# Splitting the tokens for the expert gather inside the routing stage, on ScalarE and VectorE

## The chip, the cores and the metric

The kernel runs on one core of one Trainium2 chip. The metric is the device time of one execution in microseconds (us); three runs of the kernel before took 749.75, 750.12 and 750.17, median 750.12. Beside them stands one execution taken with the hardware profiler, from which all durations below are read. Times in rows count from the start of its span.

The engines are named TensorE (PE in the rows; PEld is its weight load), VectorE (DVE), ScalarE (ACT), GpSimd (POOL) and SyncE (SP). SyncE issues nearly all transfers; they run on 16 DMA engines.

## The reference

One decoder layer on 256 tokens of width 1024, in float32. First a mixer (two attention branches of 8 heads, gates, an output projection), then the part that the change is in, a mixture of 64 experts with hidden width 256, of which each token takes 8:

```python
h2 = modulate(rms_norm(x, norm2_g), shift2, scale2)      # 256 x 1024 tokens
scores = sigmoid(h2 @ w_router)                          # 256 x 64
choice = scores + router_bias
# 4 of 8 groups by the sum of their two best, then the 8 best experts in them
wts = scores at the chosen experts, normalised, times 2.5
y[token] = sum over its 8 experts of
           wts * (silu(h2 @ w_gate_e) * (h2 @ w_up_e)) @ w_down_e
y += swiglu of the shared expert, on all tokens
x = x + gate2 * y
out = rms_norm(x, final_g)
```

Each expert has three matrices of 1 MB, 64 x 3 MB in all, and each must be read once.

## The kernel before, in words

The kernel has three stretches. The mixer runs to about 240 us. The routing stage follows, in which the tokens are normalised, scored and assigned, and the shared expert's first product is formed. Then comes the expert stage, 26 tiles of 128 slots each.

A tile holds the slots of two experts (64 + 64, or 96 + 32) or of four (32 each). The first three tiles take experts 0 to 5, whose weights can be loaded before the routing is known; the later tiles take experts in the order of their counts, and their loads read the expert's number from the tensor `order`, which SyncE loads into registers (line 1093). For each tile there are a matrix `S` of ones and zeros, token by slot (`slots`, line 1039, made on VectorE by comparing places), a gather of the tokens (`gather`, line 1058), the gate and up product (`tile_up`, line 1122, into the one PSUM buffer `gu`), a turn of the hidden values (`hidden_T`), the down product (`down`, line 1169) and the scatter into the four accumulators (line 1185). The scatter and the next gather stand between a tile's gate and up product and its down product; in tile 0 the next gather stands behind the down product.

The gather is a matrix product of tokens with `S`. From tile 1 on it runs in bfloat16, on three parts of each token that add up to it: `hp3[t][0]`, `[1]` and `[2]` for the two halves t of the 256 tokens. Part 0 is h2 rounded, part 1 the rounded rest, part 2 the rest of the rest. `part` (line 1031) makes them, a copy on ScalarE and a subtraction on GpSimd in each of four calls; the rest lies in the buffer `sr` (`r1`). h2 itself lies in the buffer `gr0` and is read there in steps of eight elements. Tile 0's gather takes h2 in float32 instead, with `S` in float32, so that it needs no parts: 32 products instead of 48.

The weights go into a ring of 1 MB buffers, `ring` (line 121 and 798). `w8()` takes the next name in it; each expert takes three: half of gate and up, the other half, and down. The ring begins with vv and the nine w8 buffers; then come whi, whi, wlo, wlo, hh, g2r, xs and gr1, buffers of the mixer and the routing that come free one after the other, and before tile 3 gr0 and sr are put in front (line 1272). In the rows gr0 and gr1 both read `gr`. The shared expert takes the first two, tiles 0, 1 and 2 the next 18.

The order of work on TensorE, VectorE, ScalarE and SyncE is the order of the program text (`manual_schedule`, line 194): an engine executes its instructions in that order, and waits at the first one whose inputs or whose buffer are not ready. In the mixer a list of steps, `plan`, gives that order. SyncE's queue holds the loads in the order of the tiles, and a load whose buffer is in use holds all that are behind it. Beside that each load waits until an earlier one has landed.

In the routing stage, from line 1205, the shared expert's products (`shared_up`) are cut into pieces between the steps of the routing: `choose` picks the experts of one half of the tokens (VectorE), `places` counts the slots (TensorE, then VectorE), `rank` and `expert_order` make `order`, `choice_weights` the weights. `residual` copies x into the accumulators on ScalarE, after which xs is free.

Of the kernel before, what the change touches and what calls it, by code (L numbers as in the profile page):

```python
# [21 lines left out]
NT = 2  # L22
# [86 lines left out]
def block_kernel(ctx: ExitStack, tc: tile.TileContext, x, c, norm1_g, norm2_g, w_ada, b_ada, w_in,  # L109
# [63 lines left out]
    def tokens_T(t, place):  # L173

        for half in range(2):
            p = place()
            for b in range(4):
                nc.tensor.transpose(p[:, b * 128:(b + 1) * 128], h2v[t][:, 4 * half + b, :], ident)
            nc.scalar.activation(h2T[0][:, half * 4:half * 4 + 4, t * 128:(t + 1) * 128],
                                 p.rearrange("p (b q) -> p b q", b=4), AF.Copy)  # L180

    lgs = {}
# [12 lines left out]
    with ExitStack() as pa:  # L195
# [473 lines left out]
        def channel_tiles():  # L669
            h = k8("gr0", [P, NT, D])  # L670
            h2.extend(h[:, t] for t in range(NT))
            h2v.extend(h[:, t].rearrange("q (p j) -> q j p", j=8) for t in range(NT))
            r1.extend(a.rearrange("p (j q) -> p j q", j=8) for a in (sr[:, 0], sr[:, 1]))
            h2T.append(k8("gr1", [P, 8, 256]))
            pack = k8("qksb3", [P, 4, NT, NE])
            scores_.extend(pack[:, i] for i in range(4))
# [4 lines left out]
        def do(f, *args, keys=()):  # L681
            plan.append((keys, lambda: f(*args)))
# [95 lines left out]
        do(outp, 1, 0, 1)  # L778
        do(tokens_T, 0, att)
        do(outp, 1, 4, 1)  # L780
        do(router, 0, att)
# [16 lines left out]
    ring.insert(0, "vv")  # L798
    ring.extend(["whi", "whi", "wlo", "wlo", "hh", "g2r", "xs", "gr1"])
    hp3.extend([k8(f"qk{n}{k}", [P, 8, P], BF) for k in range(3)] for n in ("sb", "mb"))  # L800
    ps = ctx.enter_context(tc.tile_pool(name="ps2", bufs=1, reuse_waits="tile", space=PSUM))
# [228 lines left out]

    def part(t, k):

        src = h2v[t] if k == 0 else r1[t]
        nc.scalar.activation(hp3[t][k], src, AF.Copy)
        nc.gpsimd.tensor_tensor(hp3[t][2] if k else r1[t], src, hp3[t][k], op=OP.subtract)

    xgb = []

    def slots(i, dtype=BF):

        entries = TILES[i]
        S = wk.tile([P, NT, 128], dtype, name="S", tag="zs", bufs=4)
        for t in range(NT):
# [14 lines left out]
    def gather(i, S):  # L1058
        if not xgb:
            xgb.append(k8("hl", [P, 2, 8, 128]))  # L1060
        xg = xgb[0][:, i % 2]

        parts = h2v if i == 0 else [hp3[t][k] for t in range(NT) for k in range(3)]
        n = len(parts)
        for half in range(2):
            p = rot()
            for b in range(4):
                for k in range(n):
                    mm(p[:, b * 128:(b + 1) * 128], parts[k][:, half * 4 + b, :], S[:, k * NT // n], start=k == 0,  # L1069
                       stop=k == n - 1)  # L1070
            dst = xg[:, half * 4:half * 4 + 4].rearrange("p b s -> p (b s)")
# [132 lines left out]

    load_shared()
    shared_up(0, 0, 5)
    tokens_T(1, rot)
# [3 lines left out]
    scores(1)  # L1211
    choose(0)
    choose(1)
    nc.scalar.preload_act_table_set("silu_and_others")
    for t in range(NT):
        for half in range(2):
            residual(t, half)
    shared_up(1, 0, 2)
    places()
    S = slots(0, F32)  # L1220
    shp[0] = swiglu(shp[0])
    shared_up(1, 2, 8)
    shp[1] = swiglu(shp[1])
    xg = gather(0, S)
    part(0, 0)
    part(1, 0)
    rank()
    expert_order()
    choice_weights()
    part(0, 1)  # L1230
    part(1, 1)

# [37 lines left out]
    for i in range(len(TILES)):  # L1270
        if i == 3:
            ring[:0] = ["gr0", "sr"]
        if i == SH_AT:
# [58 lines left out]
```

## Time and profile before

| | |
|---|---|
| median of three runs | 750.12 us (749.75 to 750.17) |
| the profiled execution, its own time | 748.62 us |
| its span, first to last instruction | 746.5 us |
| mean granted clock of TensorE | 0.987 of full |
| TensorE busy | 696.3 us, 93% of the span |
| VectorE busy | 312.3 us, 42% |
| ScalarE busy | 202.3 us, 27% |
| GpSimd busy | 25.1 us, 3% |
| DMA | 266.73 MB, mean 357 GB/s |
| chain that ended last | TensorE 53%, DMA 41%, VectorE 2%, ScalarE 1% |

A row of the timeline gives a start, a busy time, the engine, the line of the kernel, and what is written from what; the brackets at its end tell how long the engine sat idle before, and whom it waited for. TensorE's busy time is no measure of how near it is to its peak, since matmuls are pipelined. The engine with the most busy time doesn't bound every stage: in the routing stage one reads which wait ends last. SPq is SyncE's queue; a row there is the issue of a transfer, not the transfer.

### The profile page before, as it was taken

To read this page: it belongs to the slowest core of one execution; us is meant where nothing else is said; L and a number is where in the kernel's file an instruction comes from. 1 tells how busy PE (TensorE), PEld (TensorE's weight loads), DVE (VectorE), ACT (ScalarE), POOL (GpSimd) and SP (SyncE) were. 2 spreads that over 40 slices of the span, in tenths; PEclk is the share of its full clock that TensorE was granted. 3 is DMA by queue.
4 is the path that set the end of the run, shared out by engine and by line. 5 is a ranking of instruction groups with operands and counts; after the bars stand their busy time and mean duration, and the time that the engine had idled before them with its cause. 6 is when DMAs were issued, how large, how long until landed. Compare 5 with 4: busy or idle time off the path is not lost.

```text
span 746.5 us, 12489 instructions
## 1 busy us (share of the span) xinstructions
PE 696.3 (93%) x4727; PEld 389.5 (52%) x4727; DVE 312.3 (42%) x663; ACT 202.3 (27%) x332; POOL 25.1 (3%) x37
## 2 busy tenths in 40 slices
PE   3799999999999979999999999999999998899994
PEld 0486677667787645544444444444444453445532
DVE  1365766766667342333333233332242332223323
ACT  2354665465743231111111111011111110111122
POOL 1010001000001050000000000000000000000000
PEclk9999999999999998999999999999999999999998
DMA  9999988776658659999999999999999999999994
GB/s 352 412 380 389 375 285 301 253 270 217 240 210 297 250 216 383 375 382 413 409 414 413 413 410 396 411 411 412 415 412 412 413 412 414 406 410 412 406 333 157
DMA packets 76862, 266.73 MB, mean 357 GB/s; under 512 B 7013, under 2 KB 9221, under 8 KB 67968
## 3 DMA queue, kind: packets, MB, share of 16 engines
q1 hardware_dynamic: 75344, 262.24, 90.9%
q0 software_dynamic: 1312, 3.65, 1.5%
q8 instruction: 39, 0.64, 0.3%
q14 instruction: 23, 0.19, 0.1%
q10 hardware_dynamic: 144, 0.00, 0.0%
HBM read 264.68 MB, written 1.19 MB: 356 GB/s over the span
## 4 chain that ended last, share of the span: by engine, by line
PE 53%; DMA 41%; DVE 2%; ACT 1%; SPq 1%; issue 1%; POOL 1%; DVEq 0%; ACTq 0%
PE gu L1129 9%; PE big L264 7%; PE big L267 7%; PE big L265 7%; DMA w<-in_w_up_e_dram 6%; DMA w<-in_w_gate_e_dram 5%; DMA whi<-in_w_gate_e_dram 5%; PE rot L1069 5%; PE rot L1153 4%; DMA w<-in_w_ada_dram 3%; DMA whi<-in_w_down_e_dram 3%; PE acc L1185 3%; DMA g2r<-in_w_gate_e_dram 3%; DMA vv<-in_w_down_e_dram 2%; PE att L412 2%; DMA g2r<-in_w_up_e_dram 2%
## 5 line engine op out<-in xcount | busy, mean ns | idle before, releaser
L1129 PE MATMUL gu<-w,hl 128*32 128x512 f32 (+1 forms) x552 | 108.1, 594 | 1.5 <-DMA w<-in_w_up_e_dram 1.4
L264 PE MATMUL big<-whi,hh 128*128 128x512 f32 x184 | 75.0, 408 | 1.7 <-ACT whi L384 1.7
L1153 PE MATMUL rot<-w,at 128*32 128x512 f32 (+1 forms) x272 | 69.6, 629 | 5.7 <-DVE at L1008 5.7
L265 PE MATMUL big<-whi,hl 128*128 128x512 f32 x184 | 72.6, 395 | 0.0
L993 DVE TENSOR_TENSOR sg<-sg,gu 128x256 f32<-128x256 f32 x27 | 11.4, 421 | 140.5 <-ACT sg L992 140.5
L1165 ACT ACTIVATE mg<-y 128x512 fp32r<-128x512 f32 x51 | 32.1, 630 | 130.4 <-DVE y L1159 130.4
L1069 PE MATMUL rot<-S,qksb 128*128 128x128 bf16 x600 | 66.4, 219 | 0.0
L1159 DVE SCALAR_TENSOR_TENSOR y<-rot,wsl,gate 128x512 f32<-128x512 f32 (+1 forms) x53 | 39.1, 738 | 65.0 <-PE rot L1153 63.8
L1069 PE MATMUL rot<-S,qkmb 128*128 128x128 bf16 x600 | 66.1, 219 | 0.0
L1129 PEld LDWEIGHTS gu<-w,hl 128*32 128x32 f32 (+1 forms) x552 | 32.3, 121 | 57.5 <-issue 53.2
L246 DVE TENSOR_TENSOR wlo<-w,whi 128x2048 fp32r<-128x2048 f32 x23 | 52.7, 2291 | 20.1 <-ACT whi L245 19.1
L267 PE MATMUL big<-wlo,hh 128*128 128x512 f32 x184 | 54.0, 394 | 0.2 <-DVE wlo L246 0.2
L1185 PE MATMUL acc<-mg,ST 128*128 128x512 f32 x204 | 54.1, 406 | 0.0
L1166 DVE TENSOR_TENSOR mg<-y,mg 128x512 fp32r<-128x512 f32 x51 | 35.3, 693 | 38.5 <-ACT mg L1165 38.5
L1073 ACT ACTIVATE hl<-rot 128x512 f32<-128x512 f32 x26 | 15.5, 597 | 127.9 <-PE rot L1069 127.9
L992 ACT ACTIVATE sg<-gu 128x256 f32<-128x256 f32 x27 | 10.3, 383 | 136.1 <-PE gu L1129 136.1
L1185 PEld LDWEIGHTS acc<-mg,ST 128*128 128x128 f32 x204 | 36.3, 188 | 17.4 <-ACT sg L992 9.1
L245 ACT ACTIVATE whi<-w 128x2048 fp32r<-128x2048 f32 x23 | 43.9, 1910 | 5.0 <-PE big L265 5.0
L1069 PEld LDWEIGHTS <-qksb 128*128 128x128 bf16 x600 | 40.9, 98 | 7.2 <-issue 6.1
L264 PEld LDWEIGHTS big<-whi,hh 128*128 128x128 f32 x184 | 34.9, 190 | 17.1 <-issue 3.8
L1069 PEld LDWEIGHTS <-qkmb 128*128 128x128 bf16 x600 | 42.0, 98 | 0.0
L1129 PE MATMUL gu<-gr,hl 128*64 128x512 f32 (+1 forms) x104 | 39.6, 593 | 0.5 <-DMA gr<-in_w_up_e_dram 0.5
(354 smaller groups left out, 1103.8 us busy)
## 6 DMA issues: line engine op xcount, KB each, us to landing
w<-in_w_gate_e_dram SPq DMA_DIRECT2D x58, 512.0 KB, 12.0
w<-in_w_up_e_dram SPq DMA_DIRECT2D x58, 512.0 KB, 12.3
w<-in_w_down_e_dram SPq DMA_DIRECT2D x28, 1024.0 KB, 12.0
w<-in_w_ada_dram SPq DMA_DIRECT2D x24, 1024.0 KB, 12.5
w<-in_w_in_dram SPq DMA_DIRECT2D x16, 1024.0 KB, 13.0
whi<-in_w_gate_e_dram SPq DMA_DIRECT2D x12, 512.0 KB, 11.9
whi<-in_w_up_e_dram SPq DMA_DIRECT2D x12, 512.0 KB, 12.1
wlo<-in_w_down_e_dram SPq DMA_DIRECT2D x6, 1024.0 KB, 11.3
```

Of the source, the lines that this page charges most:

```text
L245: nc.scalar.activation(hi, w, AF.Copy)
L246: nc.vector.tensor_tensor(lo, w, hi.bitcast(F32), op=OP.subtract)
L264: mm(p, aa[i][0], ww[i][0], start=start and i == 0, stop=False)
L265: mm(p, aa[i][1], ww[i][0], start=False, stop=False)
L267: mm(p, aa[i][0], ww[i][1], start=False, stop=stop and i == n - 1)
L1069: mm(p[:, b * 128:(b + 1) * 128], parts[k][:, half * 4 + b, :], S[:, k * NT // n], start=k == 0, stop=k == n - 1)
L1129: mm(p[c0:c0 + n, :], xg[:, j, c0:c0 + n], gu[s][j], start=j == 0, stop=j == 7, skip_group_check=True)
L1153: mm(py[c0:c0 + w, 0:n], at[:, jj, c0:c0 + w], wd[s][:, jj, o:o + n], start=jj == 0, stop=jj == 1, skip_group_check=True)
L1159: nc.vector.scalar_tensor_tensor(y, py[:, 0:n], wsl, gate2[:, o:o + n], op0=OP.mult, op1=OP.mult)
L1165: nc.scalar.activation(yh, y, AF.Copy)
L1166: nc.vector.tensor_tensor(yl, y, yh.bitcast(F32), op=OP.subtract)
L1185: mm(sums(t, c), m if len(y) > 1 else m.bitcast(F32), part, start=False, stop=stop and k == len(y) - 1, skip_group_check=True)
```

## The change

`part` is cut in two: the copy stays on ScalarE (`part`), the subtraction goes from GpSimd to VectorE (`part_rest`). Both are defined in the mixer's scope, and their calls are spread over the routing stage, the first one (`part(0, 0)`) in the mixer's plan. Tile 0's gather now takes the six bfloat16 parts like every other tile's, and its `S` is bfloat16. `rank` stands before the gather, and the residual copies stand behind the swiglu of the shared expert. In the ring gr0, gr1, sr and xs follow g2r from the start, where xs and gr1 stood, and nothing is put in before tile 3.

```diff
+    def part(t, k):
+        nc.scalar.activation(hp3[t][k], r1[t] if k else h2v[t], AF.Copy)
+    def part_rest(t, k):
+        nc.vector.tensor_tensor(hp3[t][2] if k else r1[t], r1[t] if k else h2v[t], hp3[t][k], op=OP.subtract)
...
         do(tokens_T, 0, att)
+        do(part, 0, 0)
         do(outp, 1, 4, 1)
...
-    ring.extend(["whi", "whi", "wlo", "wlo", "hh", "g2r", "xs", "gr1"])
+    ring.extend(["whi", "whi", "wlo", "wlo", "hh", "g2r", "gr0", "gr1", "sr", "xs"])
...
-    def part(t, k):
-        src = h2v[t] if k == 0 else r1[t]
-        nc.scalar.activation(hp3[t][k], src, AF.Copy)
-        nc.gpsimd.tensor_tensor(hp3[t][2] if k else r1[t], src, hp3[t][k], op=OP.subtract)
...
-        parts = h2v if i == 0 else [hp3[t][k] for t in range(NT) for k in range(3)]
...
-                for k in range(n):
-                    mm(p[:, b * 128:(b + 1) * 128], parts[k][:, half * 4 + b, :], S[:, k * NT // n], start=k == 0,
-                       stop=k == n - 1)
+                for k in range(6):
+                    mm(p[:, b * 128:(b + 1) * 128], hp3[k // 3][k % 3][:, half * 4 + b, :], S[:, k // 3],
+                       start=k == 0, stop=k == 5)
...
     load_shared()
+    part(1, 0)
     shared_up(0, 0, 5)
     tokens_T(1, rot)
...
     choose(0)
+    part_rest(0, 0)
     choose(1)
+    part(0, 1)
     nc.scalar.preload_act_table_set("silu_and_others")
+    shared_up(1, 0, 2)
+    places()
+    S = slots(0)
+    shared_up(1, 2, 8)
+    part_rest(1, 0)
+    part(1, 1)
+    part_rest(0, 1)
+    part_rest(1, 1)
+    for t in range(NT):
+        shp[t] = swiglu(shp[t])
+    rank()
     for t in range(NT):
         for half in range(2):
             residual(t, half)
-    shared_up(1, 0, 2)
-    places()
-    S = slots(0, F32)
-    shp[0] = swiglu(shp[0])
-    shared_up(1, 2, 8)
-    shp[1] = swiglu(shp[1])
     xg = gather(0, S)
-    part(0, 0)
-    part(1, 0)
-    rank()
     expert_order()
     choice_weights()
-    part(0, 1)
-    part(1, 1)
...
-        if i == 3:
-            ring[:0] = ["gr0", "sr"]
```

Two places show how the instructions move. The first is VectorE's order from the places of the tokens to the copy of tile 0's gather, before. Here qksb_1804 holds the places, gu and the first rot the shared expert's products, the second rot the gathered tokens:

```order
L858 SCALAR_TENSOR_TENSOR qksb_1804<-rot,seld 128x128
L1052 TENSOR_TENSOR S<-ca,qksb_1804 128x128 x2
L993 TENSOR_TENSOR sg<-sg,gu 128x256
L993 TENSOR_TENSOR sg<-sg,rot 128x256
L1075 COPY hl<-rot 128x512
L866 SCALAR_TENSOR_TENSOR kr<-rot,ca 64x64
L868 COPY cnt<-rot 64x1
```

And the same place now, where qksb_1805 holds the places, gr_1802 is h2, and qksb_1939, qksb_1940, qkmb_1941, qkmb_1942 and qkmb_1943 are parts of the tokens:

```order
L869 SCALAR_TENSOR_TENSOR qksb_1805<-rot,seld 128x128
L1057 TENSOR_TENSOR S<-ca,qksb_1805 128x128 x2
L188 TENSOR_TENSOR sr<-gr_1802,qkmb_1941 128x1024
L188 TENSOR_TENSOR qksb_1940<-sr,qksb_1939 128x1024
L188 TENSOR_TENSOR qkmb_1943<-sr,qkmb_1942 128x1024
L1004 TENSOR_TENSOR sg<-sg,gu 128x256
L1004 TENSOR_TENSOR sg<-sg,rot 128x256
L877 SCALAR_TENSOR_TENSOR kr<-rot,ca 64x64
L879 COPY cnt<-rot 64x1
L880 SCALAR_TENSOR_TENSOR kc<-cnt,ca 64x1
L882 TENSOR_SCALAR kr,kc<-kr,kc 64x64
L884 TENSOR_SCALAR gbm<-ca,kc 64x64
```

Three of the four subtractions now stand between S and the shared expert's swiglu, and the ranking stands ahead of the gather's copy. The fourth subtraction, part_rest(0, 0), stands between the two choices, further up.

The second place is SyncE's queue from g2r on, before. These are the last loads of tile 2, and the loads of `order` into registers that tile 3 begins with:

```order
L162 DMA g2r<-in_w_gate_e_dram 128x1024
L163 DMA g2r<-in_w_up_e_dram 128x1024
L162 DMA xs<-in_w_gate_e_dram 128x1024
L163 DMA xs<-in_w_up_e_dram 128x1024
L162 DMA gr_2420<-in_w_gate_e_dram 128x1024
L163 DMA gr_2420<-in_w_up_e_dram 128x1024
L168 DMA vv<-in_w_down_e_dram 128x2048
L168 DMA w_2425<-in_w_down_e_dram 128x2048
L1093 TENSOR_LOAD order
```

And now, where gr_2449 is gr0 and gr_2452 is gr1:

```order
L162 DMA g2r<-in_w_gate_e_dram 128x1024
L163 DMA g2r<-in_w_up_e_dram 128x1024
L162 DMA gr_2449<-in_w_gate_e_dram 128x1024
L163 DMA gr_2449<-in_w_up_e_dram 128x1024
L162 DMA gr_2452<-in_w_gate_e_dram 128x1024
L163 DMA gr_2452<-in_w_up_e_dram 128x1024
L168 DMA sr<-in_w_down_e_dram 128x2048
L168 DMA xs<-in_w_down_e_dram 128x2048
L1095 TENSOR_LOAD order
```

Tile 2 now ends in gr0, gr1, sr and xs, and tile 3 begins with vv and w, where it began with gr0 and sr.

## Rows read from the trace of the kernel before

**Rows 1.** Busy us of PE, PEld, DVE, ACT, POOL by stretch; clock, DMA share, GB/s.

```profile
250.00:280.00 30.00, 26.23 (x110) 14.98 (x111) 11.08 (x41) 9.93 (x14) 10.10 (x5) 0.95 0.56 196
290.00:340.00 50.00, 48.44 (x396) 24.53 (x396) 16.00 (x39) 6.09 (x11) 0.00 (x0) 1.00 1.01 388
340.00:440.00 100.00, 96.90 (x940) 46.01 (x934) 33.44 (x79) 13.46 (x24) 0.00 (x0) 1.00 1.02 412
```

**Rows 2.** SyncE's queue by time: start and busy us of each issue.

```profile
251.97 0.33 SPq L162 DMA_DIRECT2D xs<-in_w_gate_e_dram  x1
...
257.39 0.33 SPq L162 DMA_DIRECT2D gr<-in_w_gate_e_dram  x1
...
272.83 0.35 SPq L162 DMA_DIRECT2D gr<-in_w_gate_e_dram  x1
...
277.09 0.33 SPq L162 DMA_DIRECT2D sr<-in_w_gate_e_dram  x1
...
305.97 0.34 SPq L162 DMA_DIRECT2D wlo<-in_w_gate_e_dram  x1
```

**Rows 3.** Waits of SyncE's queue, 240 to 290: total, times, longest us.

```profile
SPq L162 <- ACT sg L992: 8.4, 1, 8.4
...
SPq L162 <- POOL sr L1035: 4.7, 1, 4.7
```

**Rows 4.** GpSimd by time, the first of four subtractions.

```profile
267.52 2.67 POOL L1035 TENSOR_TENSOR sr<-gr,qksb 128x1024 f32<-128x1024 f32 x1 [1.24 <-ACT qksb L1034]
```

**Rows 5.** TensorE by time, tile 0 and the start of tile 1.

```profile
257.20 7.65 PE L1069 MATMUL rot<-S,gr 128*128 128x128 f32 x32
...
265.09 3.65 PE L1129 MATMUL gu<-w,hl 128*64 128x512 f32 x16
...
269.23 3.65 PE L1129 MATMUL gu<-w,hl 128*64 128x512 f32 x16
...
279.35 5.96 PE L1153 MATMUL rot<-w,at 128*64 128x512 f32 x16
...
288.18 3.72 PE L1129 MATMUL gu<-w,hl 128*64 128x512 f32 x16
```

**Rows 6.** The chain that ended last: start, us, what.

```profile
272.84 1.06 ACT qkmb L1034
...
274.88 2.33 DVE S L1052 x2
...
278.56 0.87 PE rot L936 x2
...
315.51 2.70 PE rot L1069 x48
...
351.47 12.54 DMA whi<-in_w_gate_e_dram
```

**Rows 7.** VectorE by time.

```profile
227.94 0.69 DVE L649 TENSOR_TENSOR mg<-big,sr 128x512 f32<-128x512 f32 x1
...
248.51 0.23 DVE L831 TENSOR_TENSOR tmp<-qksb,biasr 128x64 f32<-128x64 f32 x1 [2.58 <-ACT qksb L190]
...
252.38 0.49 DVE L1052 TENSOR_TENSOR S<-ca,qksb 128x128 f32<-128x128 f32 x2
...
262.77 0.19 DVE L874 CAST permb<-gbm 64x64 bf16<-64x64 f32 x1
```

**Rows 8.** Busy us in one stretch (columns of rows 1), the clock third from last.

```profile
278.00:279.00 1.00, 0.81 (x3) 0.39 (x2) 0.76 (x4) 0.00 (x0) 0.00 (x0) 0.50 0.92 266
```

**Rows 9.** ScalarE by time.

```profile
236.42 1.07 ACT L179 ACTIVATE gr<-att 128x512 f32<-128x512 f32 x2
240.17 0.63 ACT L657 ACTIVATE mg<-xs 128x512 f32<-128x512 f32 x1 [2.68 <-DVE xs L650]
...
245.23 1.08 ACT L179 ACTIVATE gr<-rot 128x512 f32<-128x512 f32 x2 [2.47 <-PE rot L178]
...
249.79 2.15 ACT L1029 ACTIVATE acc<-xs 128x512 f32<-128x512 f32 x4
...
265.38 2.06 ACT L1034 ACTIVATE qksb<-gr 128x1024 bf16<-128x1024 f32 x1
```

## What was predicted

> **What bounds the kernel now.** I read the busy time by stretch first, to see where the weight stream is not full. In the expert stage the DMA moves 412 GB/s from 340 to 440 [rows 1]; in the 30 us of routing, 250 to 280, it moves 196. That stretch alone misses (412 - 196) x 30 / 412 = 15.7 us of transfer. Behind it, from 290 to 340, it still misses (412 - 388) x 50 / 412 = 2.9 us. The expert stage is the stream: whatever the stream is late when it becomes full, the end is late.
>
> Then SyncE's queue, to see why it is not full. The queue issues in program order and stops at the first buffer that is not free. It gets xs at 251.97, gr1 at 257.39, then nothing until gr0 at 272.83 and sr at 277.09, and from there buffer after buffer [rows 2]. Its waits name the releasers: 8.4 us for ScalarE before xs, and 4.7 us for a GpSimd subtraction on sr [rows 3]. GpSimd takes 2.67 us for one subtraction [rows 4] and has four in a row, after ScalarE's copies.
>
> Then TensorE in the same stretch: the float32 gather of tile 0 takes 7.65 us, tile 0's gate and up run in two halves from 265.09 and 269.23, its down product comes only at 279.35 and takes 5.96, and tile 1 starts at 288.18 [rows 5]. The chain shows what lies between 272.9 and 279.35: ScalarE's last copy, then two compares for S that take 2.33 us together [rows 6], where the same two took 0.49 at 252.38 [rows 7]. GpSimd's subtractions run beside the slow ones. The clock is at half (1.2 GHz) at 278 to 279 [rows 8], after the wait, and the down product pays for it: its 16 products take 5.96, where 16 of the same width in the half before took 3.65 [rows 5]. So two things have to come earlier: the stream's restart, and TensorE's start on tile 1. From tile 1 on the chain runs through TensorE (its gather at 315.51 is one row of it), and changes at 351.47 to the DMA [rows 6]: which of the two sets the end is close.
>
> **The change part by part.** *ScalarE's four copies.* A strided one (from h2) costs 2.06 [rows 9], one from sr 1.06 [rows 6]. The first goes into an idle 2.68 us that end at 240.17, the second into an idle 2.47 that end at 245.23 [rows 9], in which the second half's h2 becomes ready at about 243.0: 243.0 + 2.06 = 245.06. The third stands behind the second scores, which come at 248.5 [rows 7], when the next work of ScalarE is copies that only SyncE's xs waits for. So all three cost nothing. Should the second start later, the turned tokens, the router and all behind them are late by the same, some tenths. Only the fourth is near the path.
>
> *VectorE's four subtractions*, instead of GpSimd's. The trace has none of this size on VectorE. Bounds: a 512-column one takes 0.69 [rows 7], so 1024 in order cost at most 1.4; I take 1.3. Of the two that read h2 in steps of eight elements the floor is that 1.3, the ceiling GpSimd's 2.67. Nearest is ScalarE's row on the very same tile, where the stride doubled the time; I take 2.4. The Trainium skill, page "SBUF — State Buffer", in the section on the DMA port swizzle, says that reads staying in one 16-byte line run at full rate and each step to a new line pays. ScalarE's two rows agree; for VectorE no run here shows it. By it the strided subtraction costs about 2.4, without it 1.3, and the start of tile 0 would come 0.5 us earlier without it.
>
> The first subtraction fits VectorE's idle 2.58 us before the second choice [rows 7]. The others stand behind S, which ends at 252.87: second subtraction 252.9 to 255.3; ScalarE's copy of it to 256.4; third 255.3 to 256.6; fourth 256.6 to 257.9. The shared product ends at about 257.4, so tile 0's gather waits some 0.5 us.
>
> *Term A, tile 0's gather.* 48 bfloat16 products take 2.70 in a later tile [rows 6], against 7.65, of which about 7.5 follow the shared product [rows 5]. Start 257.95, end 260.65. The swiglu products and the ranking now stand on VectorE before the gather's copy: 2 x 0.4 (an estimate, from 0.69 for twice the columns), then 1.25 of ranking (before, it began behind the copy of the gather's first half, 257.2 + 7.65 / 2 + 0.69 = 261.7, and ended with the cast at 262.77, 262.96 [rows 7]). From 257.9 that is 260.0, and the copy ends near 260.7; the order's products add 0.3 on TensorE. Tile 0 starts at about 261.0 instead of 265.09: -4.1. Floor: subtractions at 1.3, -4.7; ceiling: all four at GpSimd's durations, -2.
>
> *Term B, the wait before tile 0's down product.* 269.23 + 3.65 = 272.88 to 279.35 is 6.47. S falls from 2.33 to 0.49, -1.84; ScalarE's silu no longer stands behind a copy that ends at 273.90 [rows 6], -1.1; the products of the expert ranks between, 0.87 [rows 6] at half clock, take half of it, -0.4. Together -3.3. Floor and ceiling: -4.5 (only the short operations left) and -1.8 (S alone).
>
> *Term C, the clock in the down product.* 5.96 to 3.65 [rows 5]: -2.3, if the wait that B leaves (3.1 us) no longer brings the clock down. Otherwise 0.
>
> TensorE's start on tile 1: 288.18 - 4.1 - 3.3 - 2.3 = 278.5, -9.7.
>
> *The stream.* A buffer is 1.049 MB, 2.55 us at 412 GB/s. SyncE's order behind g2r was xs, gr1, vv, w, gr0, sr; now gr0, gr1, sr, xs, vv, w. The first is a loss: gr0 is free at 255.3 where xs was at 251.97. Then gr1 at 257.4 (the shared product, unchanged), sr at 257.9 (the fourth subtraction), xs when ScalarE's four residual copies (2.15 [rows 9]) are done. They now stand behind the second silu, 257.8, so 260.0. Behind xs in SyncE's queue stand the loads of the expert order; the order itself is cast at about 261.1. What the four register loads take no row prices; they fitted before 272.83, so they take less than 7 us, and vv comes at 268 at the worst, 263.7 if they take 2.6. Needed is vv at 255.3 + 4 x 2.55 = 265.5. So the sixth buffer follows at 255.3 + 5 x 2.55 = 268.05, where it was issued at 277.09: -9.0 (at worst -6.3, with 1.3 us subtractions -10.1). What is late next: buffers of tile 0, whose first two come free in the middle of tile 0 at 264.7 and are needed at 270.6, and its down weights at 275.1 for 280.8. Both in time. Later rounds have the same 20 buffers with other names.
>
> *The sum.* TensorE -9.7, stream -9.0. TensorE's release of buffers causes some of the misses from 290 to 340 (wlo only at 305.97, when tile 1's down product is over [rows 2]); coming 0.7 us more than the stream, it closes a little of them. I take -9.5. The profiled execution took 748.62 (span 746.5 and 2.1 around it): 739.1. The runs shown have a median of 750.12, 1.5 above it; measured likewise I forecast 740.6. Own range 738.5 to 742.
>
> **The rivals.**
>
> *The clock stays low.* For: TensorE had a wait of 6.5 us before the down product and ran that at half clock. Against: the wait is halved, and S no longer stands beside GpSimd. Price: term C gone, 2.3, and some of the next gather, which at half clock would take 2.7 more; I take 3 in all. TensorE is then only 6.7 earlier, the stream is ahead of it, and up to 351 the chain runs through TensorE: 743.5.
>
> *Only the gather counts.* If S and silu are late for another reason than GpSimd and ScalarE, B and C go, and TensorE gains A alone: 746.0. Against: the same two compares took 0.49 once and 2.33 beside GpSimd.
>
> *Given back.* The 20 buffers let the stream run ahead only until TensorE frees them; if TensorE's pace from 290 on set the end by itself, an earlier stream would only wait. Against: TensorE also starts earlier, and from 351 on the chain goes through the DMA. 750.1.
>
> *Slower.* The subtractions that read h2 are held on VectorE. The first stands ahead of the second choice, on the path of places, S and gather, the second behind S. Were they held as S was beside GpSimd (2.33 for 0.49, 4.75 times), each would take 2.4 x 4.75 = 11.4: the first delays the stage by 11.4 - 2.5, the second by 11.4 - 2.4, together 17.9, against 9.5 gained: 750.1 + 8.4 = 758.5. It decides from where both overruns make up the gain, 7.2 us each. Against: what held S was GpSimd's reading, and GpSimd has no tensor left to subtract there.
>
> **How the numbers follow.** Forecast 0.74, clock 0.12, gather alone 0.06, given back 0.04, slower 0.04. Below, the misses of 290 to 340 could close wholly, -2.9 more: 737.7. Above, the clock's 743.5 and part of the way to 746. Range 737.5 to 745.0. Three runs of before lie within 0.06%, so I count 0.2% (1.5 us) as a difference: faster is the first three cases, 0.92; within 0.2% the fourth, 0.04; slower 0.04.
>
> **What would show it.** Right: no GpSimd tensor work after 238; the gather of tile 0 in 2.7 us from about 258; down of tile 0 near 271.5, in 3.65, with the clock full from 250 to 290; tile 1 at 278.5; gr0 issued at 255.3, vv by 265.5; from 260 to 280 near 400 GB/s. Wrong: strided subtractions far from 2.4; a half clock after 268; a gap in SyncE's queue behind xs longer than 5 us; or a full stream from 258 and still an end above 745, which would mean that the expert stage has a pace of its own.

## The result, and the profile after

The changed kernel takes 740.11 us, the median of four runs (737.64 to 740.37); the kernel before, beside it, 749.93 (748.60 to 750.17). The ratio is 0.9851, 95% interval 0.9822 to 0.9879. The forecast was 740.6, in a range from 737.5 to 745.0. Run again twice as a control beside the experiments, the changed kernel took 738.45 and 740.48, ratios 0.9858 (0.9841 to 0.9875) and 0.9872 (0.9854 to 0.9890).

The profiled execution took 740.37, its span is 738.6. Its mixer happened to end 0.93 us later than in the profile of before: the load into hh, the last buffer that the mixer itself frees, is issued at 239.64 and not 238.71. Where the text compares moments of two profiles "from hh's issue", this shift is taken off; the starts in the table and the stretches are as the profile has them.

VectorE by time, the work between the choices and the gather's copy (start, us, then engine, line, operation, out<-in and shapes):

```profile
246.78 2.01 DVE L188 TENSOR_TENSOR sr<-gr,qksb 128x1024 f32<-128x1024 f32 x1
249.45 0.23 DVE L842 TENSOR_TENSOR tmp<-qksb,biasr 128x64 f32<-128x64 f32 x1 [0.67 <-ACT qksb L198]
...
253.72 2.01 DVE L188 TENSOR_TENSOR sr<-gr,qkmb 128x1024 f32<-128x1024 f32 x1
255.64 1.22 DVE L188 TENSOR_TENSOR qksb<-sr,qksb 128x1024 bf16<-128x1024 f32 x1
256.85 1.22 DVE L188 TENSOR_TENSOR qkmb<-sr,qkmb 128x1024 bf16<-128x1024 f32 x1
...
269.84 0.49 DVE L1057 TENSOR_TENSOR S<-ca,qksb 128x128 bf16<-128x128 f32 x2
```

The strided subtractions take 2.01, those in order 1.22. The first lies in the idle time before the second choice, of which 0.67 is left, where there were 2.58 [rows 7]. The last two compares for S are back at 0.49, where they took 2.33 [rows 6]. GpSimd has no subtraction of the tokens left. All it does between 236 and 400 is its last piece of the normalisation, over at 238.04, and the issue of the order:

```profile
236.74 1.30 POOL L667 TENSOR_TENSOR gr<-xs,g2r 128x512 f32<-128x512 f32 x1 [4.95 <-DVE xs L658]
261.85 0.56 POOL L922 DMA_DIRECT2D order_d<-order  x1 [23.81 <-DVE qksb L927]
```

TensorE by time, the answer to [rows 5]. In front stands the gather of tile 0, from the chain that ended last (start, us, what):

```profile
258.29 2.68 PE rot L1071 x48
```

```profile
261.21 3.65 PE L1131 MATMUL gu<-w,hl 128*64 128x512 f32 x16
...
265.36 3.65 PE L1131 MATMUL gu<-w,hl 128*64 128x512 f32 x16
...
271.97 5.27 PE L1155 MATMUL rot<-w,at 128*64 128x512 f32 x16
...
280.42 3.72 PE L1131 MATMUL gu<-w,hl 128*64 128x512 f32 x16 [0.39 <-DVE hl L1077]
...
294.53 3.65 PE L1155 MATMUL rot<-wlo,at 128*64 128x512 f32 x16
```

The gather takes 2.68 instead of 7.65, the gap before the down product is 271.97 - 269.01 = 2.96 instead of 6.47, and tile 1 starts at 280.42 instead of 288.18. The down product is still slow, 5.27, and the granted clock is at half there (0.50 of full, 1.2 GHz, from 272 to 273 in the rows further down), though the gap before it is halved. SyncE's queue (start and busy us of the first issue of each load), the answer to [rows 2]:

```profile
255.87 0.33 SPq L162 DMA_DIRECT2D gr<-in_w_gate_e_dram  x1
258.37 0.33 SPq L162 DMA_DIRECT2D gr<-in_w_gate_e_dram  x1
259.29 0.36 SPq L168 DMA_DIRECT2D sr<-in_w_down_e_dram  x1
260.79 0.33 SPq L168 DMA_DIRECT2D xs<-in_w_down_e_dram  x1
264.27 0.35 SPq L162 DMA_DIRECT2D vv<-in_w_gate_e_dram  x1
...
298.20 0.34 SPq L162 DMA_DIRECT2D wlo<-in_w_gate_e_dram  x1
```

No gap of 15 us is left in it. The last row is the one that matters later: wlo is issued as soon as tile 1's down product (294.53 + 3.65 = 298.18), which reads it, is over. That is a load that waits for TensorE to give a buffer back. Busy time by stretch (columns of rows 1; GB/s last, the clock third from last):

```profile
250.00:280.00 30.00, 29.03 (x191) 14.07 (x189) 17.13 (x58) 8.39 (x15) 0.56 (x1) 0.94 0.79 295
250.00:290.00 40.00, 38.64 (x237) 19.01 (x235) 18.71 (x62) 9.38 (x17) 0.56 (x1) 0.96 0.85 325
272.00:273.00 1.00, 1.00 (x5) 0.38 (x6) 0.42 (x1) 0.38 (x1) 0.00 (x0) 0.50 1.06 356
290.00:340.00 50.00, 48.44 (x429) 23.15 (x428) 17.04 (x41) 6.72 (x12) 0.00 (x0) 1.00 1.00 383
340.00:440.00 100.00, 96.90 (x904) 46.03 (x903) 33.42 (x76) 13.45 (x24) 0.00 (x0) 1.00 1.02 412
```

And the second of these stretches before:

```profile
250.00:290.00 40.00, 36.15 (x181) 19.95 (x182) 14.56 (x46) 12.07 (x17) 10.10 (x5) 0.91 0.67 236
```

From these rows comes the account used below. At 412 GB/s the stream would carry 40 or 50 us of weights in the two stretches; what it carried less, in us, is (412 - rate) x length / 412. This is called missing time here. Before: (412 - 236) x 40 / 412 = 17.1 up to 290, and 2.9 from 290 to 340 [rows 1], together 20.0. After: 8.4 and 3.5, together 12.0. From 340 to 440 both run at 412. So 8.0 us less are missing, and the span is 7.9 us shorter: the time went out of the stream's pauses. Which of two things makes the pauses end is the question of the experiments: buffers that the routing stage frees late (theory S: the stream's restart sets the end), or buffers that TensorE, running through the tiles, gives back late (theory R: TensorE's start on tile 1 sets the end).

### The profile page after: what moved, and what is told of

Same layout as the page of the kernel before. It is cut to its first block, busy times and chain, and to the rows that moved or that the text cites. A ratio compares the mean times of both kernels' runs of the same rounds, so it can differ in the third digit from the quotient of the medians.

```text
span 738.6 us, 12518 instructions
## 1 busy us (share of the span) xinstructions
PE 691.3 (94%) x4743; PEld 384.3 (52%) x4743; DVE 316.2 (43%) x667; ACT 202.2 (27%) x332; POOL 16.0 (2%) x33
## 3 DMA queue, kind: packets, MB, share of 16 engines
q0 software_dynamic: 1312, 3.65, 1.5%
## 4 chain that ended last, share of the span: by engine, by line
PE 51%; DMA 45%; DVE 2%; ACT 1%; issue 0%; SPq 0%; DVEq 0%; ACTq 0%
DMA w<-in_w_up_e_dram 17%; PE gu L1131 9%; PE big L272 7%; PE big L275 7%; PE big L273 7%; DMA wlo<-in_w_up_e_dram 7%; DMA sr<-in_w_down_e_dram 5%; PE rot L1155 4%; DMA w<-in_w_down_e_dram 4%; DMA hh<-in_w_down_e_dram 4%; DMA w<-in_w_ada_dram 4%; PE rot L1071 3%; DMA gr<-in_w_up_e_dram 3%; PE acc L1187 3%; PE att L420 2%; DMA hh<-in_w_gate_e_dram 2%
## 5 line engine op out<-in xcount | busy, mean ns | idle before, releaser
L1131 PE MATMUL gu<-w,hl 128*32 128x512 f32 (+1 forms) x568 | 99.0, 594 | 2.4 <-DMA w<-in_w_up_e_dram 2.0
L1004 DVE TENSOR_TENSOR sg<-sg,gu 128x256 f32<-128x256 f32 x27 | 11.4, 421 | 138.7 <-ACT sg L1003 138.7
L1071 PE MATMUL rot<-S,qksb 128*128 128x128 bf16 x624 | 69.1, 219 | 0.0
L1071 PE MATMUL rot<-S,qkmb 128*128 128x128 bf16 x624 | 68.7, 219 | 0.0
L1131 PEld LDWEIGHTS gu<-w,hl 128*32 128x32 f32 (+1 forms) x568 | 29.9, 121 | 60.9 <-issue 58.8
L1155 PE MATMUL rot<-w,at 128*32 128x512 f32 (+1 forms) x256 | 56.2, 610 | 5.7 <-DVE at L1019 5.7
L1071 PEld LDWEIGHTS <-qksb 128*128 128x128 bf16 x624 | 42.6, 98 | 7.8 <-issue 6.7
L272 PEld LDWEIGHTS big<-whi,hh 128*128 128x128 f32 x184 | 35.1, 191 | 17.1 <-issue 3.8
L1071 PEld LDWEIGHTS <-qkmb 128*128 128x128 bf16 x624 | 43.6, 98 | 0.0
L275 PEld LDWEIGHTS big<-wlo,hh 128*128 128x128 f32 x184 | 34.8, 190 | 8.4 <-DVE wlo L254 0.6
## 6 DMA issues: line engine op xcount, KB each, us to landing
whi<-in_w_up_e_dram SPq DMA_DIRECT2D x12, 512.0 KB, 11.7
```

What stands on the lines that cost most here:

```text
L272: mm(p, aa[i][0], ww[i][0], start=start and i == 0, stop=False)
L275: mm(p, aa[i][0], ww[i][1], start=False, stop=stop and i == n - 1)
L1071: mm(p[:, b * 128:(b + 1) * 128], hp3[k // 3][k % 3][:, half * 4 + b, :], S[:, k // 3], start=k == 0, stop=k == 5)
L1131: mm(p[c0:c0 + n, :], xg[:, j, c0:c0 + n], gu[s][j], start=j == 0, stop=j == 7, skip_group_check=True)
L1155: mm(py[c0:c0 + w, 0:n], at[:, jj, c0:c0 + w], wd[s][:, jj, o:o + n], start=jj == 0, stop=jj == 1, skip_group_check=True)
```

## The experiments

All are edits of the changed kernel, but for e7, an edit of the kernel before. The table has the median of the timed runs, and from the profile of each the start of tile 1 on TensorE, the span's end behind that start, and the missing us in the two stretches, worked out as above from the rows of each.

| run | time | tile 1 | end behind it | missing to 290 | 290 to 340 | span - missing |
|---|---|---|---|---|---|---|
| before | 749.93 | 288.18 | 458.3 | 17.1 | 2.9 | 726.5 |
| after | 740.11 | 280.42 | 458.2 | 8.4 | 3.5 | 726.6 |
| c_after | 738.45 | 277.76 | 457.6 | 7.3 | 2.4 | 725.7 |
| c_after2 | 740.48 | 279.23 | 459.9 | 8.0 | 2.4 | 728.7 |
| e1 | 740.81 | 279.72 | 457.9 | 12.7 | -0.1 | 725.0 |
| e2 | 738.19 | 278.15 | 457.8 | 7.2 | 2.4 | 726.3 |
| e3 | 739.57 | 278.06 | 459.1 | 7.1 | 2.9 | 727.2 |
| e4 | 737.78 | 277.79 | 458.1 | 7.9 | 1.3 | 726.7 |
| e5 | 744.19 | 283.00 | 458.7 | 11.7 | 3.3 | 726.8 |
| e6 | 742.19 | 282.40 | 458.0 | 11.2 | 2.5 | 726.7 |
| e7 | 746.35 | 285.51 | 458.6 | 14.9 | 2.1 | 727.2 |
| e8 | 745.78 | 284.42 | 458.8 | 8.4 | 7.5 | 727.2 |
| e9 | 752.36 | 277.90 | 473.4 | 23.3 | 0.1 | 727.9 |
| e10 | 739.55 | 278.05 | 459.2 | 11.0 | -0.1 | 726.4 |

The last column holds within 2 us of 727 while the spans go from 735.4 to 751.3: the end moves with what the stream misses up to 340. This is bookkeeping (each run reads the same weights, and behind 340 at nearly the same rate); it tells where the time went, not what caused it. The end lies 457.6 to 459.9 behind the start of tile 1 in all runs but e9.

**c_after, c_after2: the changed kernel again.**

> The changed kernel again, as the measure for the three beside it. Theory R (TensorE's release of weight buffers sets the end: tile 1 began 7.8 us earlier in the changed profile, 8.7 after taking off a mixer that ended 0.9 us later) and theory S (the restart of the weight stream sets the end) both expect the ratio measured so far, 0.985 of the kernel before, about 9 to 10 us less.

> The changed kernel once more, as the control for the runs beside it: 738.5, within 1.5 us; tile 1 starts at 277.7 to 278.5, and the end lies 457.5 to 459 us behind it.

738.45 and 740.48: the second lies 0.5 us outside what was expected of it, and its profile starts tile 1 at 279.23 and ends 459.9 behind that, both later than expected. Medians of one kernel differ by 2 us here, and profiles by the mixer's end (hh at 238.63 and 240.10) and by the clock. So differences of 2 us and less are read from moments within the profiles, if at all. In both controls the down product takes 3.65 at full clock, in the first profile of the same kernel 5.27. e1 to e3 ran beside c_after, e8 to e10 beside c_after2; e4 to e7 had no run of the changed kernel beside them.

**e1: the old ring order**, with the new copies and gather. xs, now freed by the residual copies behind the swiglu, leads the ring again.

```diff
-    ring.extend(["whi", "whi", "wlo", "wlo", "hh", "g2r", "gr0", "gr1", "sr", "xs"])
+    ring.extend(["whi", "whi", "wlo", "wlo", "hh", "g2r", "xs", "gr1"])
...
+        if i == 3:
+            ring[:0] = ["gr0", "sr"]
```

> The changed kernel with the ring order of the kernel before: after g2r come xs and gr1, and gr0 and sr are put in front before tile 3. xs is free only behind the residual copies, 260.8 instead of gr0 at 255.9, so the stream restarts 4.9 us later; TensorE's work is unchanged. Theory S: about 4 to 5 us slower than the changed kernel. Theory R: the stream has some 3.5 us of misses from 290 to 340 in which it waits for TensorE, and these take up most of the delay: 0 to 1.5 us slower, and the misses from 290 to 340 shrink.

740.81, ratio to before 0.9885 (0.9870 to 0.9900), 2.4 us over its control, whose interval ends at 0.9875; from c_after2 it is not told apart. The 2.4 lie outside both expected ranges, 4 to 5 and 0 to 1.5. The queue stands still until xs comes free:

```profile
260.09 0.33 SPq L162 DMA_DIRECT2D xs<-in_w_gate_e_dram  x1
...
266.04 0.35 SPq L162 DMA_DIRECT2D gr<-in_w_gate_e_dram  x1
```

```profile
250.00:290.00 40.00, 38.64 (x246) 19.35 (x245) 18.08 (x55) 8.70 (x16) 0.56 (x1) 0.96 0.74 281
290.00:340.00 50.00, 48.45 (x424) 23.14 (x422) 17.74 (x43) 6.72 (x12) 0.00 (x0) 1.00 1.02 413
```

The stream misses 5.4 us more than c_after up to 290, and nothing behind: the 2.4 us that c_after misses there are gone. The end lies as far behind tile 1's start as ever, which looks like theory R alone. But the clock was at half in this profile's down product (5.28), and tile 1 started 1.65 us later than in c_after (40.78 from hh's issue for 39.13). Both sides moved, so e1 doesn't decide.

**e2: useless products that hold the clock**, three before tile 0's hidden turn, six in the wait before its down product.

```diff
+        fill(p[:, 256:512], 6)
...
-        at = hidden_T(sg)
+        at = hidden_T(sg, n=0 if i else 3)
```

> The changed kernel with 9 products of no use put into TensorE's waits before tile 0's down product (3 before its turn, 6 while the ranks wait), so that the clock should not fall there; the stream's buffers are untouched. In the changed profile the clock is at half from 272 to 275.3 and the down product takes 5.27 us instead of 3.6. If activity holds the clock: the down product in 3.6, tile 1 about 1.7 us earlier. Theory R: 1 to 1.7 us faster than the changed kernel. Theory S: no difference. If the clock falls all the same, neither is tested and the waits are not what brings it down.

738.19, 0.9844 (0.9830 to 0.9857), not told apart from the 738.45 beside it. The clock was full in both, so this run says nothing on what the filler does, and tests neither theory.

**e3: xs first and early.** The residual copies go up to where they were, ahead of `places`.

```diff
-    ring.extend([... "g2r", "gr0", "gr1", "sr", "xs"])
+    ring.extend([... "g2r", "xs", "gr0", "gr1", "sr"])
```

> The changed kernel with the residual copies moved up into ScalarE's 4.1 us idle stretch before the fourth copy of the tokens, and with xs put right behind g2r in the ring. The stream restarts at about 253.9 (xs free) instead of 255.9; gr0, gr1 and sr follow, then vv at 264.3, so the stream is 2 us earlier until there; TensorE's work is unchanged. Theory S: 1.5 to 2 us faster than the changed kernel. Theory R: no difference beyond 0.5 us, the stream waits that much longer for TensorE at the end of tile 1's and tile 2's down products.

xs is issued at 253.14; from hh's issue that is 2.0 us before the first load of its control. 739.57, 0.9872 (0.9856 to 0.9888): no gain. But the lead was gone long before 290: up to there the stream misses 7.1, for 7.3 in c_after. It was lost from 268 to 272, where the DMA ran at 320 and 334 GB/s, for 412 and 399. From 262 to 278 the queue waited for earlier loads to land, and for TensorE only 0.2 us. So this earlier restart brings nothing, but the queue shows no wait for TensorE there, which theory R would need, and e3 doesn't decide either.

**e4: tile 1's gather moved into the wait** before tile 0's down product.

```diff
         nc.vector.tensor_copy(posmr, p[:, 0:2 * NE].rearrange("p (t e) -> p t e", t=2))
+        xgs.append(gather(1, S))
...
-                xg = gather(i + 1, S)
+                xg = xgs[0]
```

> The changed kernel with tile 1's gather moved into TensorE's wait before tile 0's down product: behind the first products of the ranks instead of behind the down product. The parts it needs are ready there now. Nothing changes for the stream's first ten buffers. The gather's 2.7 us cover some 1.0 us in which TensorE waits and the copy that tile 1 waits for, so tile 1 starts about 1.5 us earlier. Theory R (TensorE's start on tile 1 sets the end; so far the end came 457.6 to 459.1 us behind it in every profile): 1 to 1.5 us faster than the changed kernel, end again about 458 behind tile 1's start. Theory S (restart of the stream): no difference.

737.78, 0.9844 (0.9824 to 0.9863). From hh's issue to tile 1 it is 38.57 us, 0.56 less than in c_after and not the 1.5 that were expected; a difference of that size is below what the times can show, so e4 tests neither theory.

**e5: tile 0's gather from h2 in float32 again**, as before the change, with S in float32 too, and with gr0 last in the ring, since the gather reads it.

```diff
-                for k in range(6):
+                for k in range(n):
...
+        parts = h2v if i == 0 else [hp3[t][k] for t in range(NT) for k in range(3)]
```

> The changed kernel with tile 0's gather back in float32 from h2 (32 products, S in float32); since h2 then is read until the gather ends, the ring is g2r, gr1, sr, xs, gr0, so that the loads behind don't wait for gr0 too early. The subtractions stay on VectorE and in their places. Term A is undone: tile 0 starts 4 to 5 us later. Theory R: tile 1 starts 4 to 5 us later and the time is 4 to 5 us above the changed kernel, so that the gather's form is about half of the gain. Theory S: the stream restarts at 257.4 instead of 254.9 but halts again at gr0 near 265 and at vv near 268: 3 to 5 us, so this run doesn't tell R and S apart, it gives the size of the term.

744.19, 0.9936 (0.9917 to 0.9956). By the ratios that is 4.8 us over c_after2 and 5.8 over c_after. Its gather:

```profile
257.57 7.65 PE L1073 MATMUL rot<-S,gr 128*128 128x128 f32 x32
265.46 3.65 PE L1133 MATMUL gu<-w,hl 128*64 128x512 f32 x16
```

Tile 1 starts 43.92 behind hh's issue, 4.8 later than in the controls. So the bfloat16 gather with its ring order is worth about half of the gain.

**e6: the four subtractions on GpSimd**, in the places of the changed kernel.

```diff
-        nc.vector.tensor_tensor(hp3[t][2] if k else r1[t], ...
+        nc.gpsimd.tensor_tensor(hp3[t][2] if k else r1[t], ...
```

> The changed kernel with the four subtractions back on GpSimd, called in the same places. GpSimd can begin the first when its copy is done, 240.4, and the second at 246, earlier than VectorE, so gr0 comes free about 5 us earlier. Theory of contention (what slowed S from 0.49 to 2.33 us before): the normalisation of the second half and the choices, on VectorE beside it, are slowed, the routing takes 2 to 5 us longer, tile 1 starts that much later, and under R the time is 2 to 5 us above the changed kernel although the stream restarts earlier. Rival, that only the place of the work matters and not the engine: the same as the changed kernel within 0.5 us; under S even 2 to 4 us faster.

742.19, 0.9907 (0.9882 to 0.9933). By the ratios that is 2.6 us over c_after2, whose interval it touches, and 3.7 over c_after. In the profile tile 1 starts 42.81 behind hh's issue, 3.7 later than in both. First GpSimd by time, then VectorE:

```profile
240.43 3.06 POOL L188 TENSOR_TENSOR sr<-gr,qksb 128x1024 f32<-128x1024 f32 x1 [2.43 <-ACT qksb L184]
247.84 2.63 POOL L188 TENSOR_TENSOR sr<-gr,qkmb 128x1024 f32<-128x1024 f32 x1 [4.34 <-ACT qkmb L184]
251.58 2.12 POOL L188 TENSOR_TENSOR qksb<-sr,qksb 128x1024 bf16<-128x1024 f32 x1 [1.11 <-ACT qksb L184]
253.95 2.12 POOL L188 TENSOR_TENSOR qkmb<-sr,qkmb 128x1024 bf16<-128x1024 f32 x1 [0.24 <-ACT qkmb L184]
```

```profile
241.04 3.00 DVE L667 TENSOR_TENSOR gr<-xs,g2r 128x512 f32<-128x512 f32 x1
...
248.34 2.18 DVE L854 TENSOR_SCALAR gbm<-tmp 128x64 bf16<-128x64 f32 x1
...
252.33 1.40 DVE L849 TENSOR_SCALAR tmp<-tmp 128x8 f32<-128x8 f32 x1
...
254.03 0.23 DVE L852 MAX8 tmp<-tmp 128x8 f32<-128x64 f32 x1
254.29 0.09 DVE L853 MATCH_VALUE_LOAD tmp<-tmp 128x8 f32 x1
254.37 0.21 DVE L853 MATCH_REPLACE8 tmp<-tmp 128x64 f32<-128x64 f32 x1
254.61 1.51 DVE L854 TENSOR_SCALAR gbm<-tmp 128x64 bf16<-128x64 f32 x1
```

Beside GpSimd's four subtractions VectorE operations that take 0.69, 0.20, 0.17 and 0.20 in the changed kernel take 3.00, 2.18, 1.40 and 1.51. The last three end where GpSimd's ends: 248.34 + 2.18 = 250.52 against 247.84 + 2.63 = 250.47, then 253.73 against 253.70, and 256.12 against 256.07; the first, with 0.69 of work of its own, ends 0.55 behind (244.04, 243.49). This reads as being held until the other is over, not as being slowed by a factor. Not every operation is held: the MAX8 and the MATCH_REPLACE8 above lie within the last subtraction and take what they take in the changed kernel.

S in the kernel before fits that reading. Its two compares end at 274.88 + 2.33 = 277.21 [rows 6], and GpSimd's last subtraction there at 274.85 + 2.22 = 277.07:

```profile
274.85 2.22 POOL L1035 TENSOR_TENSOR qkmb<-sr,qkmb 128x1024 bf16<-128x1024 f32 x1
```

This wait is what the change took out of the stage.

**e7: the kernel before with only the subtractions on VectorE**, behind `choice_weights`; ScalarE's copies stay where they were.

```diff
+    part_rest(0, 0)
     part(0, 1)
+    part_rest(1, 0)
     part(1, 1)
+    part_rest(0, 1)
+    part_rest(1, 1)
```

> The kernel before with one part of the change alone: the subtractions on VectorE, behind the weights of the choice; gather, ring and all other places as before. Contention goes, S takes 0.49 us, but the four subtractions (2.0, 2.0, 1.2, 1.2 us) now stand on VectorE ahead of the places of tile 0's slot map. The down product of tile 0 comes about 2 us earlier, gr0 is free at 271.5 and sr at 273.9 instead of 272.8 and 277.1. Theory R: about 2 us faster than the kernel before; theory S: about 3. If the engine were most of the change, it would be 7 or more.

746.35, 0.9959 (0.9944 to 0.9974), 3.0 us less than before; 2 to 3 were expected. The strided subtractions take 2.05 and 2.03 there, those in order 1.22 and 1.23, S 0.49. Tile 1 starts 45.42 behind hh's issue, 4.05 earlier than before, and 2.3 of these come from the down product, which ran at full clock here (3.65) and at half in the profile of before (5.96). Whether the new engine or chance brought the clock up is open (see term C below), so the 3.0 are not the engine's for certain.

**e8: TensorE later, the stream's first loads as they were.** 54 useless products ahead of tile 0's down product.

```diff
+        for k in range(54):
+            mm(p[:, 256:512], identb, ..., start=True, stop=True, skip_group_check=True)
```

> The changed kernel with 54 useless products of 256 columns on TensorE ahead of tile 0's down product, about 6 us of work there; some 1.0 us of it fills a wait that is there already. The stream's first loads and their releases up to that point are left as they are. If TensorE's start on tile 1 sets the end: tile 1 starts 4.5 to 5.5 us later, the end is later by the same, and the end again lies 457.5 to 459 us behind that start; about 743.5 to 744. If the stream's restart sets the end: the time of the changed kernel, 738.5, within 1 us.

745.78, 0.9954 (0.9938 to 0.9969), 5.3 us over c_after2 beside it, where theory R had expected 4.5 to 5.5 and theory S at most 1. TensorE by time, then the busy time by stretch:

```profile
270.94 6.07 PE L945 MATMUL rot<-qksb,identb 128*128 128x256 bf16 x54
...
284.42 3.72 PE L1133 MATMUL gu<-w,hl 128*64 128x512 f32 x16 [0.39 <-DVE hl L1079]
```

```profile
250.00:290.00 40.00, 39.30 (x271) 21.78 (x272) 17.91 (x61) 9.35 (x16) 0.56 (x1) 1.00 0.85 325
290.00:340.00 50.00, 48.44 (x414) 23.82 (x414) 17.39 (x40) 6.72 (x12) 0.00 (x0) 1.00 0.92 350
```

Tile 1 starts 5.2 us later than in c_after2, the end comes with it (458.8 behind that start), and nearly all of it shows as stream missing behind 290, 7.5 for 2.4. This is what theory R says, and it speaks against S alone: the stream's restart was the same, 16.2 us behind hh's issue in both.

**e9: the stream later, TensorE as it was.** xs first in the ring, and the residual copies that free it behind tile 0's silu.

```diff
-    ring.extend([... "g2r", "gr0", "gr1", "sr", "xs"])
+    ring.extend([... "g2r", "xs", "gr0", "gr1", "sr"])
...
+            if i == 0:
+                for t in range(NT):
+                    for half in range(2):
+                        residual(t, half)
```

> The changed kernel with xs as the first buffer behind g2r and the residual copies, which free it, behind tile 0's silu: the stream stands still until about 270.5 instead of 255.9, about 15 us later; TensorE's work and order are unchanged. If the stream's restart sets the end: 15 us later, about 753. If TensorE's start on tile 1 sets it: nothing until the stream's slack is used up, of which the old ring order has shown at least 5 us; tile 2 and 3 then wait for weights, and the time is 738.5 + (15 - slack), 744 to 749 for a slack of 5 to 10 us, with the end farther than 459 us behind tile 1's start by that same amount.

752.36, 1.0033 (1.0019 to 1.0046), 11.9 us over c_after2; theory S had expected 753, theory R 744 to 749. SyncE's queue, TensorE, and the stretches:

```profile
270.68 0.33 SPq L162 DMA_DIRECT2D xs<-in_w_gate_e_dram  x1
```

```profile
277.90 3.72 PE L1131 MATMUL gu<-w,hl 128*64 128x512 f32 x16 [0.39 <-DVE hl L1077]
```

```profile
250.00:290.00 40.00, 38.64 (x278) 20.67 (x277) 17.99 (x54) 8.53 (x16) 0.56 (x1) 1.00 0.46 172
290.00:340.00 50.00, 48.44 (x418) 22.89 (x416) 17.96 (x44) 6.72 (x12) 0.00 (x0) 1.00 1.02 411
```

TensorE starts tile 1 in time, and the end lies 473.4 behind it. The stream misses 15.3 us more than c_after2 up to 290, and gets 2.3 back behind: 13.0 more in all. Slack is the delay that the stream can take before the end moves; it comes out at 2.3 us by the missing time and at 3.4 by the times (15.3 - 11.9). That is about what the changed kernel's stream misses behind 290, 2.4 to 3.5, and not the 5 to 10 that this expectation took from e1. The queue's waits show the same: from 290 to 340 it waits 13.2 us for down products (line 1155) in c_after2 and 0.3 in e9, so that here the stream no longer waits for TensorE. From 337 on TensorE waits for the stream instead, 9.2 us for loads into w before its gate and up products, where it waits 1.7 in c_after2. Theory R doesn't hold alone: once the slack is used up, the stream's restart sets the end.

**e10: TensorE earlier once more**, with e4's gather, the ranking behind the copy of tile 0's gather, and the order's products in the middle of tile 0.

```diff
-    rank()
     for t in range(NT):
...
     xg = gather(0, S)
-    expert_order()
+    rank()
...
-            sg = tile_up(i, xg, gu, () if i else [by_expert])
+            sg = tile_up(i, xg, gu, () if i else [expert_order, by_expert])
```

> The changed kernel with tile 1's gather put into the wait before tile 0's down product, the ranking behind the copy of tile 0's gather, and the expert order's products in the middle of tile 0. If TensorE's start on tile 1 sets the end: that start comes 1 to 1.5 us earlier than in the changed kernel, about 276.5, and the time is 737.2, 1 to 1.5 us less. If the stream sets it: the order, and with it the first buffer behind the four, comes some 2.4 us later, and the time is up to 2.4 us more, 740.9.

739.55, 0.9864 (0.9847 to 0.9880), not told apart from c_after2 (740.48). The order, and vv behind it, come later:

```profile
260.62 0.33 SPq L168 DMA_DIRECT2D xs<-in_w_down_e_dram  x1
267.71 0.35 SPq L162 DMA_DIRECT2D vv<-in_w_gate_e_dram  x1
```

```profile
250.00:290.00 40.00, 39.03 (x278) 19.95 (x277) 18.72 (x59) 9.21 (x17) 0.56 (x1) 1.00 0.84 299
290.00:340.00 50.00, 48.44 (x418) 22.88 (x415) 17.96 (x44) 6.72 (x12) 0.00 (x0) 1.00 1.02 413
```

From hh's issue it is 28.2 us to vv, 24.7 in c_after2, and the stream misses 3.0 us more up to 290 and nothing behind. By the account the stream is the later of the two here, and TensorE's 0.6 us (38.57 from hh's issue to tile 1) are lost. The time agrees with that but does not show it: 739.55 lies between the 737.2 and the 740.9 that were expected of the two theories. Of all versions e2 and e4 have the lowest ratio, 0.9844, but no interval parts either from the changed kernel.

## Why the prediction was right, and where it was not

*The subtractions on VectorE.* Forecast 2.4 strided and 1.3 in order; 2.01 and 1.22. The stride costs VectorE a factor of 1.65, less than ScalarE's two. So the rule that the prediction cited (the Trainium skill, page "SBUF — State Buffer", section on the DMA port swizzle) holds for VectorE too; the size that the prediction had taken from ScalarE's row was too large. The rival in which they are held, 11.4 us each, has fallen; e6 shows that GpSimd holds VectorE, and in the changed kernel GpSimd has nothing there.

*Term A.* Forecast -4.1. From hh's issue to tile 0: 26.38 before [rows 5], 21.57 after, -4.8, a tenth more than the floor of -4.7; the strided subtraction behind S is 0.4 shorter than taken, the two in order 0.2 together. The gather starts at 258.13, 257.2 with the mixer's delay taken off, for 257.95.

*Term B.* Forecast -3.3, measured 2.96 - 6.47 = -3.5.

*Term C.* Forecast -2.3 for the down product at full clock. In the first profile it was at half clock again, and 5.27 instead of 5.96 is all that came; in c_after and c_after2 it was at full, 3.65. Of the nine profiles since the change in which nothing was put into the wait (3 us, in e7 4.4), it was at half in two (after, e1) and full in seven. So the order of work alone doesn't set whether the clock falls there, and what decides it stays open. "A half clock after 268" was one of the prediction's own signs of being wrong; it was there in the first profile, and the time came within the range all the same. The rival "the clock stays low" was priced too high: the next gather, tile 1's, ran at full speed (277.17 to 280.02, 2.85, as in c_after), so only 1.65 us lie between the two ways up to tile 1, and that profile still took 740.37, not 743.5.

*TensorE up to tile 1.* Forecast -9.7. From hh's issue: 49.47 before, 40.78 after (-8.7), 39.13 in both controls (-10.3).

*The stream.* gr0 forecast at 255.3, came at 255.87, or 254.9 without the mixer's delay; vv at 264.27, or 263.3, for 263.7. Missing up to 290: 17.1 before, 8.4 after, -8.7 for -9.0, without taking off the mixer's 0.93. The four register loads and what lies around them fit into 2.4 us between the order's issue at 261.85 and vv. (The worst case in the prediction, vv at 268, gives 268 + 2.55 = 270.55 and so -6.5, not -6.3.)

*The weak step is the sum.* It took -9.0 from the stream as the base ("whatever the stream is late when it becomes full, the end is late"), and let TensorE's lead close a little of the misses from 290 to 340. They weren't closed: 2.9 before, 3.5 after, 2.4 in both controls. In the changed kernel the stream restarts 2 to 3.5 us sooner than it must (e9), and waits for TensorE from 290 on, as wlo for tile 1's down product (298.18, 298.20); a later TensorE costs its whole delay (e8). So TensorE's -8.7 to -10.3 is what was paid out, with the stream's -9.0 close behind. For the kernel before the same follows from its 2.9 missing behind 290, but no run tests it there. That the number came out right is in part luck: the sum started from the side with slack, and both sides moved by about nine microseconds; in the first profile, more gain than forecast in term A makes up part of what term C lacks. The prediction had said that which of the two sets the end is close, and the small slack in e9 bears that out: by this account, gaining on TensorE alone would have ended after some 3 us. The chain of waits passes from TensorE to the DMA at 338.60:

```profile
338.60 12.52 DMA w<-in_w_down_e_dram
```

where it did at 351.47 [rows 6]; this moment moves from profile to profile (414.02 in c_after2) and doesn't tell which side has slack. The rate from 290 to 340 does.

*The parts of the gain.* The bfloat16 gather with its ring order is worth 4.8 to 5.8 us (e5), the new engine in the new places 2.6 to 3.7 (e6). In the kernel before, the new engine is worth up to 3.0 (e7, with the clock's part in it open). The ring order alone is worth 2.4 at most (e1, with the clock at half in its profile). These need not add up to the whole, since by the account the end follows the later of two sides. "Only the gather counts" (746.0) and "given back" (750.1) have fallen by the result.

## What to carry to other kernels

Where a weight stream feeds an engine through a ring of buffers, work out both sides up to the place where the stream is full for good: what it misses before the engine starts, and what it misses while the engine already runs. Here misses of the second kind were the stream's slack: with 2.4 to 3.5 us of them the engine was the later side (e8), and where they were zero, the stream was (e9). A gain on one side counts only up to the other, so plan both and take the smaller.

## What the runs showed that was not expected

GpSimd's subtractions hold even small VectorE operations until they are over: a 128x64 TENSOR_SCALAR took 2.18 for 0.20 and a 128x8 one 1.40 for 0.17 (e6), not only the compares with two tensors as inputs from which the prediction had it. MAX8 (0.23) and MATCH_REPLACE8 (0.21) ran beside the same subtractions at their usual length. The Trainium skill, page "SBUF — State Buffer", section "Who interferes with whom", says that both held forms can contend with GpSimd and that the one that comes later is blocked until the other ends. The ends of the three TENSOR_SCALARs in e6 agree within 0.05 us.

With the same instructions in front and the same wait of 3 us, the down product ran at half clock in one profile of the changed kernel (5.27) and at full in two (3.65). That is 1.6 us; in e1 and e7 it stands between the experiment and what it was to show.
